# Two idle products of 512 columns around the first feed-forward unit of a hybrid encoder layer

## The chip, the cores and the metric

The kernel runs on one core of one Trainium2 chip. The metric is the device time of one execution in microseconds; the kernel before takes 914.95 us (median of 3 runs, 914.04 to 915.56). All matrices are float32. The engines named below are PE (TensorE, the matrix unit; its weight loads are listed as PEld), DVE (VectorE), ACT (ScalarE), POOL (GpSimd) and SP (SyncE, which issues most transfers).

## What is computed

One layer over 512 tokens of width 1024: two parallel mixers merged by gates, cross-attention over 256 memory tokens, and a gated feed-forward of width 2816. The change sits between the cross-attention and the feed-forward.

```python
def swiglu(hn, w_gate, w_up, w_down):
    return (jax.nn.silu(hn @ w_gate) * (hn @ w_up)) @ w_down
...
        merged = gate_a * (ya @ w_proj_a[i]) + gate_b * (yb @ w_proj_b[i])
        h = h + merged @ w_out[i]
        h = h + memory_cross_attention(rms_norm(h, xattn_norm_g[i]), memn,
                                       w_q[i], w_k[i], w_v[i], w_xo[i])
        h = h + swiglu(rms_norm(h, ffn_norm_g[i]), w_gate[i], w_up[i], w_down[i])
    return rms_norm(h, final_norm_g)
```

## The kernel before, in words

**Products.** Every float32 matrix is split into a rounded high part and a low part (`split`, L85 on ACT for the high part, L86 on DVE for the low one), and each product of two blocks is made as three PE products: high by high, high by low, low by high. Where the moving operand has all 512 tokens (or 512 weight columns), a PE product is 128x512; where it has half of the tokens, it is 128x256. The weights of a PE product are loaded by a load of its own (PEld), which runs while the product before it streams.

**Normalisation and turning.** Behind the attention's output projection each block of 128 token rows is added to the residual `h`, scaled to unit size, and turned on the PE so that features lie on partitions: `norm_feat` scales, and `to_feat` (L506) makes 8 transposes of 128x128 in two groups of four, each group into an auxiliary PSUM buffer `ptr`. ACT casts the group to the high part, DVE makes the low part, and ACT copies it once more into `full` (L510) for later sums. There are three auxiliary PSUM buffers (pool `paux`, tag `aux`), taken in turn; whoever takes one waits until the last reader of its former content is done. `to_feat` is not called at once but is put off with `later`, and `tick` calls it when the products issued since then amount to the time given. So the turning of the fourth and last block of rows falls into the first products of the feed-forward.

**Feed-forward.** The first 2560 columns of the gate and up projections are made in ten units of 512 columns. A unit multiplies a 2x2 block matrix by a 2x2 block matrix in seven jobs instead of eight (`product`, L1273), each job being 24 PE products of 128x256 on sums and differences of token blocks and weight blocks (numbered 1 to 7). The remaining 256 columns are made directly (`feat_block`, L350), in part among the first unit's jobs and the turning. The order of the jobs around the change is: half of the direct gate product and job 1 of the first gate unit (`px`), the rest of the gate product's first half, job 2 (`pv`), the gate product's second half, the direct up projection (`feat`, which takes two auxiliary PSUM buffers `pf0`, `pf1`), and then the loop over units, whose first pass begins with job 5 (`pq`), then job 6 (`px`), the next unit's jobs 1 and 2, and jobs 7, 4 and 3. Between job 5 and job 6 of the first pass one block of the normalised rows, `fn_hi` and `fn_lo` of the first four feature blocks and the last 256 tokens, is rewritten by a difference of blocks (`split(*fn_q(K0, T1), s3)`).

**Order.** Each engine works its own queue in order. A scheduler may reorder instructions within a queue except those marked `in_order`, which keep the program's order among themselves. Weights come by transfers from a plan that is issued a fixed number of jobs ahead; neither transfers nor plan are touched by the change.

**Names.** `ot_hi` holds the high part of the attention's output (features by tokens, 8 blocks of 512 tokens), complete long before the turning; its place is taken over by the feed-forward's gated values afterwards. `aux` gives an auxiliary PSUM buffer. `idles` at the start of the kernel makes small PE products whose results nobody reads, while the first transfers are under way. `NT - 1` is the last block of rows.

Of the kernel before, what the change touches and what calls it, by code (L numbers as in the profile page):

```python
# [17 lines left out]
P = 128  # L18
D = 1024
T = 512  # L20
NT = T // P
# [31 lines left out]
def hybrid_layer_kernel(  # L53
# [8 lines left out]
    nc = tc.nc  # L62
    x, mem, out = x[0], mem[0], out[0]
# [13 lines left out]
    def bank(name):  # L77
        return pm.tile([P, 512], F32, tag="mm", name=name)

    def aux(name, shape=(P, 512)):  # L80
        return pa.tile(list(shape), F32, tag="aux", name=name)

    def split(dst_hi, dst_lo, src):

        hi = nc.scalar.copy(dst_hi, src)  # L85
        lo = nc.vector.tensor_tensor(dst_lo, src, dst_hi.bitcast(F32), ALU.subtract)  # L86
        if pinned[0]:
            in_order(hi)
            in_order(lo)
# [3 lines left out]
    in_order = tc.keep_in_program_order  # L93
# [228 lines left out]
    def next_w(*key):  # L322
        i = used_w[0]
        used_w[0] += 1
        assert len(plan[i][0]) == len(key) and plan[i][0][1:] == key[1:] and plan[i][0][0] is key[0]
        for j in range(i, min(i + FAR + 1, len(plan))):
            begin(j, i)
            if j - 1 >= len(tiles) and j - 1 <= i + SPLITS:
                split_w(j - 1)
        for j in range(len(tiles), min(i + SPLITS + 1, len(plan))):  # L330
            split_w(j)
        tile_, tiles[i] = tiles[i], None
        return tile_
# [98 lines left out]
    def later(n, fn):  # L432

        side["later"].append((side["now"] + n, fn))
# [7 lines left out]
    def tick(us=5.2):  # L442

        side["now"] += us / 5.2
        run_due()
        side["credit"] = min(side["credit"] + us * side["rate"], us)
        while side["credit"] > 0.0 and side["gen"] is not None:
            try:
                used = next(side["gen"])
            except StopIteration:  # L450
                side["gen"] = None
                return
            if used is None:
                side["credit"] = 0.0
                return
            side["credit"] -= used

    def gain(src, name):
        t = np_.tile([P, D], F32, tag="gain", name=name, bufs=2)
        nc.sync.dma_start(t, src.partition_broadcast(P))  # L460
        return t

    ident = cp.tile([P, P], F32, name="ident")
# [6 lines left out]
    def sum_sq(dst, src):  # L470
        sq = np_.tile([P, 512], F32, tag="ev", name="sq", bufs=2)
        act = nc.scalar.activation(sq[:, :src.shape[-1]], src, AF.Square, accum_out=dst)
        if pinned[0]:
            in_order(act)
# [13 lines left out]
    def row_sums(src):  # L488
        ss = np_.tile([P, 2], F32, tag="ss", name="ss", bufs=2)
        for i in range(2):  # L490
            sum_sq(ss[:, i:i + 1], src[:, HALF[i]])
        return ss

    def rms_scale(src, g, dst, ss=None):

        r = rms_factor(row_sums(src) if ss is None else ss)
        for i in range(2):
            nc.vector.scalar_tensor_tensor(dst[:, HALF[i]], src[:, HALF[i]], r, g[:, HALF[i]], ALU.mult, ALU.mult)

    def to_feat(src, hi, lo, tsl, full=None, skip=None, part=(0, 1)):  # L500

        for q in part:
            ps = aux("ptr", (P, 4, P))
            for j in range(4):
                k = 4 * q + j
                nc.tensor.transpose(ps[:, j, :], src[:, k * P:(k + 1) * P], ident)  # L506
            if q != skip:
                split(hi[:, 4 * q:4 * q + 4, tsl], lo[:, 4 * q:4 * q + 4, tsl], ps)
            if full is not None:
                nc.scalar.copy(full[:, 4 * q:4 * q + 4, tsl], ps)  # L510

    xsp = [None]

    def norm_feat(src, g, hi, lo, tsl, ss=None, full=None, skip=None):
        xs = xsp[0].tile([P, D], F32, tag="xs", name="xs", bufs=2)
        rms_scale(src, g, xs, ss)
        later(0.6, lambda: to_feat(xs, hi, lo, tsl, full, skip))

    def slot(tag, shape, dt, name):
        return sp.tile(list(shape), dt, tag=tag, name=name)  # L520

    def token_slot(name, off=(0, 0)):

        return halves_at(sp.tile([P, 2 * KD * T + 128], F32R, tag="B", name=name), KD, T, off)
# [50 lines left out]
    ss = row_sums(xt[:, 1, :])  # L575
    for t in range(1, NT):
        rms_scale(xt[:, t, :], g_mix, xt[:, t, :], ss)
        if t == 1:
            ss = row_sums(xt[:, 2, :])
# [4 lines left out]
        if t == 2:  # L584
            ss = ss3
# [445 lines left out]
    for h in range(H):  # L1031
        ps = bank("psv")
# [22 lines left out]
    part = slot("A", (P, KD, T), F32, "part")  # L1055
# [91 lines left out]
    def add_evac(half, layer, fin, fin0=None):  # L1147

        def f(t, ps):
            nc.vector.tensor_tensor(h[:, t, HALF[half]], h[:, t, HALF[half]], ps, ALU.add)  # L1150
            sum_sq(hss[:, layer, t, half:half + 1], h[:, t, HALF[half]])
            if half == 1:
                fin(t, hss[:, layer, t, :])
            elif fin0 is not None:
                fin0(t)
        return f

    def feat_norm(g, hi, lo, full=None, skip=False):

        return lambda t, ss: norm_feat(h[:, t, :], g, hi, lo, slice(t * P, (t + 1) * P), ss, full,  # L1160
                                       0 if skip and t >= 2 else None)

    mg = (mg_hi, mg_lo)
    for half in range(2):
# [99 lines left out]
    def product(ps, u, q, start, ops):  # L1264

        hi, lo = next_w(u[0], u[1], q)
        for j in range(2):
            cs = slice(j * P, (j + 1) * P)
            for k in range(4):
                a = (hi[:, k, cs], lo[:, k, cs])  # L1270
                b = (ops[q][0][:, k, :], ops[q][1][:, k, :])
                for i, (x, y) in enumerate(((0, 0), (0, 1), (1, 0))):
                    nc.tensor.matmul(ps[:, j, :], a[x], b[y], start=start and j == k == i == 0,  # L1273
                                     stop=k == 3 and i == 2, skip_group_check=True)
        tick(2.7)

    def unit_bank(name):
        return bank(name).rearrange("p (j t) -> p j t", j=2)
# [61 lines left out]
    ot_hi = slot("D", (P, KD, T), F32R, "ot_hi")  # L1340
# [9 lines left out]
    g_f = gain(ffn_norm_g[0], "g_f")  # L1350
    ot = (ot_hi, ot_lo)
    fn_hi, fn_lo = token_slot("fn", APART)
# [9 lines left out]
    full = fp.tile([P, KD, T], F32, tag="full", name="full", bufs=1)  # L1362


    fin = add_evac(1, 1, feat_norm(g_f, fn_hi, fn_lo, full))
    held = []
    for t0 in (0, 2):
        ps = {t: bank(f"pt{t - t0}") for t in (t0, t0 + 1)}
# [51 lines left out]
    def sum4():  # L1420
        V.tensor_tensor(a12, a12, a11, ALU.add)
        make_op(3, 4, a12)
# [4 lines left out]
    def unit_start(u):  # L1427
        x, v = unit_bank("px"), unit_bank("pv")
        product(x, u, 1, True, ops)
        nc.scalar.copy(v, x)  # L1430
        return x, v
# [14 lines left out]
    ps = [bank("pf0"), bank("pf1")]  # L1446
# [61 lines left out]
    def down_product(ps, q, start, chunks=range(CHUNKS)):  # L1508
        for c in chunks:
            rows_product(ps, q, c, next_w(w_down, q, c), (0, 1), slice(0, 512), start and c == 0, c == CHUNKS - 1)  # L1510

    for i, u in enumerate(UNITS):
        final = i == len(UNITS) - 1
        x, v = begun
        q = unit_bank("pq")
        product(q, u, 5, True, ops)
        if final:
            last_job.append(u)
            make_tokens(1, 0)
        if i == 0:  # L1520
            split(*fn_q(K0, T1), s3)
        product(x, u, 6, False, ops)
        u2 = stp[0].tile([P, 2, 256], F32, tag="u2", name="u2", bufs=2)
        u3 = np_.tile([P, 2, 256], F32, tag="ev", name="u3", bufs=2)
        nc.scalar.copy(u2, x)
        if not final:
            begun = unit_start(UNITS[i + 1])
        else:
            dx = [bank(f"dx{t}") for t in range(2)]
            down_product(dx, 1, True, range(2))  # L1530
        product(x, u, 7, False, ops)
        nc.scalar.copy(u3, x)  # L1532
        if i == 0:
            sum4()
        if not final:
            unit_second(UNITS[i + 1], begun[1])
        V.tensor_tensor(u3, q, u3, ALU.subtract)
        put(u, 1, T1, u3)
        product(x, u, 4, False, ops)
        put(u, 0, T1, x)  # L1540
        if u[0] is w_up:
            a_, b_ = (acts(u[1] // 512, f)[:, :, T1] for f in (0, 1))
            V.tensor_tensor(a_, a_, b_, ALU.subtract)
        product(q, u, 3, False, ops)
        V.tensor_tensor(u2, q, u2, ALU.subtract)
        put(u, 1, T0, u2)
# [91 lines left out]
    for i in range(2):  # L1638
        p = aux("pcut", (P, 256))
# [37 lines left out]
```

## Time and profile before

| | before |
|---|---|
| time, median of 3 runs | 914.95 us (914.04 to 915.56) |
| span of the profiled execution, its own time | 915.4 us |
| weight loads (PEld) busy | 87% of the span |
| PE idle, waiting for ACT or DVE, from 589 to 800 us | none listed |
| DMA, mean | 168 GB/s |
| value projection of the attention (512 columns) | 443 to 465 us |
| query product (256 columns) | 466 to 507 us |
| turning of the last rows in front of the feed-forward | 586.4 to 587.4 us |
| units of the feed-forward (256 columns) | 608 to 804 us |
| down projection, its long run of 512 columns | 810 to 891 us |

A profile row of the timeline gives the start in us, the duration in us, the engine, the line, the operation, what is written and read, the shape and how many instructions are merged into the row. A record of a PE product is longer than its distance to the next one, because products overlap in the array; the pace has to be read from the starts, or from how many records fit into a stretch.

### The profile page before, as it was taken

Reading aid. Unit: us, or ns where it says so; the run is one execution under the profiler, and the core shown is the slowest. Engines: PE = TensorE matmul, PEld = TensorE weight load, DVE = VectorE, ACT = ScalarE, POOL = GpSimd, SP = SyncE. Lnnn points to the kernel's source line nnn. Section 1 sums busy time; section 2 is a strip of 40 time slices with the busy share of each in tenths; the row PEclk is TensorE's granted clock in tenths of the full one; section 3 lists DMA queues with packets and bytes.
Section 4 is the critical chain, followed back from the end, with each engine's and each line's share of the span. In section 5 each row is a group of like instructions: output and inputs, shape, how many; then the busy total and the mean of one; then the engine's idle time right before and its main releaser. Section 6 shows DMA issues by size and latency. Waiting matters only on the chain.

```text
span 915.4 us, 14510 instructions
## 1 busy us (share of the span) xinstructions
PE 900.7 (98%) x5650; PEld 796.5 (87%) x5650; DVE 623.8 (68%) x1018; ACT 475.4 (52%) x696; POOL 102.1 (11%) x161
## 2 busy tenths in 40 slices
PE   9999999999999999999999999999999999999996
PEld 6888888888888887789899878999999999988885
DVE  5696662888753236858956836776778767899875
ACT  5542985144364334447655634745455454655664
POOL 1004420110025200101000001100020100000000
PEclk9999999999999999999999999999999999999999
DMA  8456574685546577863578416526788873246672
GB/s 252 148 148 185 124 181 141 174 193 149 153 134 146 127 219 206 275 198 120 175 216 252 139 47 184 161 88 149 189 202 212 221 186 93 69 138 200 191 244 90
DMA packets 111974, 153.80 MB, mean 168 GB/s; under 512 B 13521, under 2 KB 78561, under 8 KB 111842
## 3 DMA queue, kind: packets, MB, share of 16 engines
q1 hardware_dynamic: 93026, 128.27, 44.1%
q0 software_dynamic: 16288, 23.57, 15.9%
q10 hardware_dynamic: 2592, 1.05, 0.5%
q8 instruction: 44, 0.72, 0.3%
q14 instruction: 24, 0.20, 0.1%
HBM read 146.08 MB, written 38.24 MB: 201 GB/s over the span
## 4 chain that ended last, share of the span: by engine, by line
PE 90%; ACT 4%; DVE 3%; issue 1%; POOL 0%; DMA 0%; POOLq 0%; SPq 0%; DVEq 0%; ACTq 0%
PE pf L350 27%; PE pt L350 16%; PE px L1273 12%; PE pq L1273 6%; PE dx L350 6%; PE dq L350 3%; PE pv L1273 3%; PE qx L1273 2%; PE dv L350 2%; PE pk L786 2%; PE ptr L506 1%; PE qq L1273 1%; DVE wlo L86 1%; PE po L350 1%; ACT whi L85 1%
## 5 line engine op out<-in xcount | busy, mean ns | idle before, releaser
L86 DVE TENSOR_TENSOR wlo<-wraw,whi 128x1024 fp32r<-128x1024 f32 (+1 forms) x139 | 164.9, 1187 | 109.5 <-ACT whi L85 107.8
L85 ACT CAST whi<-wraw 128x1024 fp32r<-128x1024 f32 (+1 forms) x139 | 142.2, 1024 | 163.0 <-PE pf L350 67.0
L350 PE MATMUL pf<-xn,whi 128*128 128x512 f32 x448 | 140.1, 392 | 0.0
L350 PEld LDWEIGHTS pf<-xn,whi 128*128 128x128 f32 x448 | 83.5, 188 | 17.0 <-issue 0.2
L350 PE MATMUL pf<-xn,wlo 128*128 128x512 f32 x224 | 87.4, 390 | 0.0
L1273 PE MATMUL px<-fn,whi 128*128 128x256 f32 x480 | 86.2, 281 | 0.0
L1273 PEld LDWEIGHTS px<-fn,whi 128*128 128x128 f32 x480 | 73.4, 188 | 0.3 <-ACT u L1532 0.2
L86 DVE TENSOR_TENSOR wlo<-b,whi 128x1024 fp32r<-128x1024 f32 x40 | 48.9, 1222 | 32.8 <-ACT whi L85 32.8
L85 ACT CAST whi<-b 128x1024 fp32r<-128x1024 f32 x40 | 42.0, 1051 | 56.2 <-PE px L1273 28.9
L1273 PE MATMUL px<-fn,wlo 128*128 128x256 f32 x240 | 67.5, 281 | 0.0
L1273 PE MATMUL pq<-s,whi 128*128 128x256 f32 x320 | 57.0, 281 | 0.0
L350 PE MATMUL dx<-whi,s 128*128 128x512 f32 x170 | 53.8, 391 | 1.4 <-ACT whi L85 1.0
L86 DVE TENSOR_TENSOR wlo<-t,whi 128x1024 fp32r<-128x1024 f32 x30 | 36.7, 1224 | 20.9 <-ACT whi L85 20.9
L85 ACT CAST whi<-t 128x1024 fp32r<-128x1024 f32 x30 | 31.5, 1051 | 36.8 <-PE pv L1273 13.3
L350 PEld LDWEIGHTS pf<-xn,wlo 128*128 128x128 f32 x224 | 42.1, 188 | 8.7
L1273 PEld LDWEIGHTS pq<-s,whi 128*128 128x128 f32 x320 | 48.9, 188 | 0.1
L1273 PEld LDWEIGHTS px<-fn,wlo 128*128 128x128 f32 x240 | 46.0, 192 | 0.0
L1273 PE MATMUL pq<-s,wlo 128*128 128x256 f32 x160 | 45.0, 281 | 0.0
L350 PE MATMUL pt<-whi,xn 128*128 128x512 f32 x128 | 42.6, 405 | 0.0
L350 PEld LDWEIGHTS dx<-whi,s 128*128 128x128 f32 x170 | 31.7, 188 | 8.3 <-ACT whi L85 1.2
L350 PE MATMUL dx<-wlo,s 128*128 128x512 f32 x85 | 33.2, 391 | 0.4 <-DVE wlo L86 0.4
L1273 PEld LDWEIGHTS pq<-s,wlo 128*128 128x128 f32 x160 | 30.7, 192 | 0.0
(414 smaller groups left out, 2235.4 us busy)
## 6 DMA issues: line engine op xcount, KB each, us to landing
wraw<-in_w_in_dram SPq DMA_DIRECT2D x36, 512.0 KB, 3.8
dsum<-in_w_down_dram SPq DMA_DIRECT2D x20, 512.0 KB, 6.7
wraw<-dsum SPq DMA_DIRECT2D x20, 512.0 KB, 4.4
b<-in_w_gate_dram SPq DMA_DIRECT2D x15, 512.0 KB, 4.6
b<-in_w_up_dram SPq DMA_DIRECT2D x15, 512.0 KB, 4.6
wraw<-in_w_down_dram SPq DMA_DIRECT2D x15, 512.0 KB, 3.7
dsum<-in_w_down_dram POOLq DMA_DIRECT2D x10, 512.0 KB, 6.8
dsum<-dsum POOLq DMA_DIRECT2D x10, 512.0 KB, 7.4
```

The lines of the kernel that those rows point to most:

```text
L85: hi = nc.scalar.copy(dst_hi, src)
L86: lo = nc.vector.tensor_tensor(dst_lo, src, dst_hi.bitcast(F32), ALU.subtract)
L350: nc.tensor.matmul(ps, a[x], b[y], start=start and i == 0, stop=stop and i == 2, skip_group_check=free)
L506: nc.tensor.transpose(ps[:, j, :], src[:, k * P:(k + 1) * P], ident)
L786: nc.tensor.matmul(ps[32 * j:32 * j + 32, q, :], bd[i][:, g].rearrange("p d c -> p (d c)"), lc(es[i], g), start=(i == 0), stop=False, tile ...
L1273: nc.tensor.matmul(ps[:, j, :], a[x], b[y], start=start and j == k == i == 0, stop=k == 3 and i == 2, skip_group_check=True)
```

## The change

A helper `long_idle` makes one PE product of 128x512 from a tile's first 128 columns as weights and its first 512 columns as the moving operand, into an auxiliary PSUM buffer that nobody reads. It is called in two places: at the end of `to_feat` for the last block of rows in front of the feed-forward, on `ot_hi`, where the transposes of this block are also marked to keep the program's order; and in the first pass over the units, between the rewriting of `fn` and job 6, on `fn_hi`. The computed result is the same.

```diff
+    def long_idle(x):
+
+        p = aux("long")
+        in_order(nc.tensor.matmul(p, x[:, 0, 0:P], x[:, 0, :], start=True, stop=True))
+
-    def to_feat(src, hi, lo, tsl, full=None, skip=None, part=(0, 1)):
+    def to_feat(src, hi, lo, tsl, full=None, skip=None, part=(0, 1), behind=None):
...
-                nc.tensor.transpose(ps[:, j, :], src[:, k * P:(k + 1) * P], ident)
+                tr = nc.tensor.transpose(ps[:, j, :], src[:, k * P:(k + 1) * P], ident)
+                if behind is not None:
+                    in_order(tr)
...
+        if behind is not None:
+            long_idle(behind)
...
-    def norm_feat(src, g, hi, lo, tsl, ss=None, full=None, skip=None):
+    def norm_feat(src, g, hi, lo, tsl, ss=None, full=None, skip=None, behind=None):
...
-        later(0.6, lambda: to_feat(xs, hi, lo, tsl, full, skip))
+        later(0.6, lambda: to_feat(xs, hi, lo, tsl, full, skip, behind=behind))
...
-    def feat_norm(g, hi, lo, full=None, skip=False):
+    def feat_norm(g, hi, lo, full=None, skip=False, behind=None):
...
-                                       0 if skip and t >= 2 else None)
+                                       0 if skip and t >= 2 else None, behind if t == NT - 1 else None)
...
-    fin = add_evac(1, 1, feat_norm(g_f, fn_hi, fn_lo, full))
+    fin = add_evac(1, 1, feat_norm(g_f, fn_hi, fn_lo, full, behind=ot_hi))
...
         if i == 0:
             split(*fn_q(K0, T1), s3)
+            long_idle(fn_hi)
         product(x, u, 6, False, ops)
```

## The prediction

> **What bounds the kernel now.** I read the page first, then the busy windows of the TensorE (PE) for stretches that hold only one kind of product, then the timeline around the two places of the change, last the waits of the feed-forward.
>
> ```profile
> span 915.4 us, 14510 instructions
> PE 900.7 (98%) x5650; PEld 796.5 (87%) x5650; DVE 623.8 (68%) x1018; ACT 475.4 (52%) x696; POOL 102.1 (11%) x161
> PEclk9999999999999999999999999999999999999999
> PE 90%; ACT 4%; DVE 3%; issue 1%; POOL 0%; DMA 0%; POOLq 0%; SPq 0%; DVEq 0%; ACTq 0%
> ```
>
> PE is busy 98% of the span and makes 90% of the chain that ended last, with the clock fully granted in every slice. So time can be won only by fewer products or by a shorter distance from one product to the next. That distance is not the same everywhere. Each row below is one stretch; its columns are the window, its length, PE's busy time with the number of records that touch it, the granted clock, the DMA engines' busy share and GB/s.
>
> ```profile
> 428.10:431.10 3.00, 3.00 (x29) 1.00 0.70 201
> 432.60:443.30 10.70, 10.70 (x93) 1.00 0.52 162
> 444.10:465.00 20.90, 20.90 (x91) 1.00 0.61 193
> 466.40:500.90 34.50, 34.50 (x307) 1.00 0.80 239
> 578.20:580.80 2.60, 2.60 (x24) 1.00 0.00 0
> 589.10:611.00 21.90, 21.90 (x188) 1.00 0.24 46
> 611.00:791.90 180.90, 180.90 (x1538) 1.00 0.69 170
> 807.20:809.90 2.70, 2.70 (x25) 1.00 0.50 123
> 810.00:891.00 81.00, 81.00 (x360) 1.00 0.67 204
> ```
>
> ```profile
> L1273 PE MATMUL qx<-hn,whi x96: 276/276/287, 465.7 to 507.0; 128*128 128x256 f32 x96
> L1273 PE MATMUL px<-fn,whi x480: 277/281/297, 578.4 to 804.6; 128*128 128x256 f32 x160
> ```
>
> A record lasts longer (276 or 281 ns) than the distance to the next, so a window touches one record's length more than it holds: distance = (window + record) / count. For products of 256 columns this is (34.50 + 0.276) / 307 = 113.3 ns in the query product stage, but (180.90 + 0.281) / 1538 = 117.8 ns in the feed-forward, and (21.90 + 0.281) / 188 = 118.0 ns in front of it. Both stages run the same helper, L1273, with weights from the same pool and rows in the same slot, at a granted clock of 1.00. Load on the DMA engines is no cause: the stretch of narrow distance has 0.80, the wide one of 578.20 has 0.00. The first two rows are the clue: both lie in the key projection, the same line and tiles, yet 428.10 has (3.00 + 0.276) / 29 = 113 ns (a short count, good to some 2 ns), and 432.60 has (10.70 + 0.281) / 93 = 118.1 ns, where the narrow distance would have fitted 97. What lies between them is only a turning of rows on the PE, after which the wide distance stays for 93 products. So there seem to be two paces, a narrow and a wide one, which an interruption sets and which then last. Products of 512 columns have two as well: (20.90 + 0.397) / 91 = 234 ns against (81.00 + 0.389) / 360 = 226 ns (0.397 and 0.389 are such records' lengths in the timeline).
>
> **The change part by part.** It removes nothing and moves no work. Instruction by instruction the queues of ACT, DVE, POOL and SP stay as they are, no DMA is added, and the PE gets two products of 128x512, whose results nobody reads. Holding the transposes in program order leaves them where they were.
>
> The first idle product comes six products into the second gate product (`pv`), behind the turning of the last 128 rows:
>
> ```profile
> 587.04 0.60 PE L506 MATMUL ptr<-ident,xs 128*128 128x128 f32 x4
> 587.39 1.19 PE L350 MATMUL pf<-fn,s 128*128 128x256 f32 x8
> 588.42 0.28 PE L1273 MATMUL pv<-fn,whi 128*128 128x256 f32 x1
> 591.24 5.82 PE L350 MATMUL pf<-fn,s 128*128 128x256 f32 x48
> 596.90 0.40 PE L350 MATMUL pf<-fn,whi 128*128 128x256 f32 x2
> ```
>
> Six products of 118 ns after 588.42 put it at 589.13. The row of 48 products gives the wide pace once more, (596.90 - 591.24) / 48 = 117.9 ns. The second one stands between job 5 and job 6 of the first unit, at 611.03:
>
> ```profile
> 610.91 0.28 PE L1273 MATMUL pq<-s,wlo 128*128 128x256 f32 x1
> 611.03 0.40 PE L1273 MATMUL px<-s,whi 128*128 128x256 f32 x2
> 586.26 0.58 ACT L510 COPY full<-ptr 128x512 f32<-128x512 f32 x1
> 588.33 1.27 ACT L510 COPY full<-ptr 128x512 f32<-128x512 f32 x2
> 606.41 1.05 ACT L85 CAST fn<-s 128x1024 fp32r<-128x1024 f32 x1
> ```
>
> Their own cost: one more place in the stream each, 226 to 234 ns by the two paces above, and the load of its weights lies under the product before it. Two make 0.46 us, all on the path.
>
> Their waits: the first needs the third auxiliary PSUM buffer back, whose last reader is the copy that ends at 586.26 + 0.58 = 586.84, 2.3 us before it. The up projection's two buffers move on by one in the ring: their last readers end at 588.33 + 1.27 = 589.60 and the first product of the up projection is at 596.90, 7.3 us later. The second reads rows that ACT has just rewritten; that cast ends at 606.41 + 1.05 = 607.46, 3.6 us before 611.03. I cost these waits at nothing. If ACT fell behind by more than those margins, everything on the PE's queue would stand behind the idle product for the excess, and the next unit's casts, which wait for the PE, with it; the trace shows nothing that would move ACT by microseconds.
>
> Their effect on the pace is the one large term, and the trace does not show a single product of 512 columns inside a wide stream of 256. If the narrow pace is reached and lasts, each later product of 256 columns saves 117.8 - 113.3 = 4.5 ns. From the second idle product to the end of the stretch there are 1538 - 2 = 1536 of them: 6.9 us. From the first there are 186 more: 7.7 us. The other bound is no gain, and below that a loss (third rival). The nearest rows for either bound are the changes from 512 to 256 columns:
>
> ```profile
> 465.26 0.40 PE L350 MATMUL pt<-wlo,mn_hi 128*128 128x512 f32 x1
> 465.50 0.39 PE L350 MATMUL pt<-whi,mn_lo 128*128 128x512 f32 x1
> 465.73 0.41 PE L1273 MATMUL qx<-hn,whi 128*128 128x256 f32 x2
> 465.97 0.28 PE L1273 MATMUL qx<-hn,wlo 128*128 128x256 f32 x1
> 466.09 0.39 PE L1273 MATMUL qx<-hn,whi 128*128 128x256 f32 x2
> 466.31 0.28 PE L1273 MATMUL qx<-hn,wlo 128*128 128x256 f32 x1
> 797.20 0.39 PE L350 MATMUL dx<-whi,s 128*128 128x512 f32 x1
> 797.42 0.40 PE L1273 MATMUL px<-fn,whi 128*128 128x256 f32 x2
> 797.66 0.28 PE L1273 MATMUL px<-fn,wlo 128*128 128x256 f32 x1
> ```
>
> At 465.73 a wide stream (233 ns per 512) turned narrow within five products (0.24 us for the first two, 0.22 for the last two). At 797.42 a stream of 512 products was followed by wide ones (0.24 us for two), and so it was at 807.20, (2.70 + 0.281) / 25 = 119 ns. So a 512 product does not set the narrow pace in every case. I take the gain: 465.73 is the nearest row in kind (the same helper, wide before it, as here), there are two tries, and nothing from 466.40 to 500.90 lost the narrow pace again over a dozen jobs of 24 products.
>
> What the faster stage would press on: casts and subtractions for the next weights.
>
> ```profile
> DVE wlo L86 <- ACT whi L85: 52.5, 46, 3.2
> ACT whi L85 <- PE px L1273: 35.2, 24, 2.0
> ```
>
> These are waits inside 589 to 800 (total us, times, longest): ACT stands waiting for the PE to give a weight buffer back, DVE for ACT, and no row there has the PE waiting. 7 us less over 200 us is 3.5%, well inside that idle time.
>
> Sum for the profiled execution: 915.4 + 0.46 - 7.7 = 908.2 if the first idle product sets the pace, 915.4 + 0.46 - 6.9 = 909.0 if only the second does. I take the middle, 908.6. The median of the runs, 914.95, lies 0.45 below that execution, so the forecast is 908.1.
>
> **The rivals.**
>
> Nothing but the cost. The wide pace is stable against a single 512 product: 797.42 and 807.20 speak for this, both in the feed-forward, where the three entries shown (578.20, 797.42, 807.20) came out wide; 465.73 speaks against. Time: 914.95 + 0.46 = 915.4. The same holds if the second product undoes at 611.03 what the first won: 186 x 4.5 ns = 0.8 us, net -0.4 us, 914.6.
> A rule points this way: the Trainium skill, "TensorE: Matmul & The Clock Gate", section "Step-by-step: what each phase is for", says that loading the next weights takes no read bandwidth from the running matmul, so there would be no pace to set. By the Trainium skill's section "Back-to-back issue gap" on that page, N/2.4 + 2.5 ns, 256 columns would take 109 ns always and two idle products of 512 together 0.43 us, an estimate that gives 915.4; the 113.3 and 117.8 ns of the rows above fit neither, so the rule is not the whole story here.
>
> Part of the way. The narrow pace is set and lost again at some unit. Against it: the wide stretch of 1538 records shows no disturbance at any unit's border. Half of the gain would give 914.95 + 0.46 - 3.8 = 911.6.
>
> Slower. The idle products leave the 256 stream wide, and shift the phase so that the down projection, now at 226 ns, enters the 234 ns pace in which the value projection (444.10) ran through all its 91 products. Price: 358 x (234 - 226) ns = 2.9 us, with the idle products 914.95 + 0.46 + 2.9 = 918.3. It decides from 810 on, where the down projection's long run of 512 columns follows the last product of 256. Against it: that entry is made today from a wide 256 stream (807.20) and ends at 226.
>
> **How the numbers follow.** Narrow pace from one of the idle products on: 0.51, 908.1. Part of the way: 0.10. Nothing but the cost, or undone: 0.23. Slower: 0.15. The rest, 0.01, is a wait that I have not seen. Differences below 0.2% (1.8 us) cannot be told from no change here, since three runs of one kernel spread over 1.5 us. So faster 0.61, same 0.23, slower 0.16. The likeliest case's own range is 907.0 to 909.3 (both sums less 0.45, and half a run's spread). The full range must take in "nothing but the cost" with its spread: 907.0 to 916.0, leaving out the slower case.
>
> **What would show it.** Right: in the changed profile products of 256 columns of the same helper lie 113.3 ns apart with records of 276 ns instead of 281, from 589.4 or 611.3 on; the unit stretch shrinks from 180.9 us to 174; two records of 128x512 without a wait in front. Wrong in the cause: records of 281 ns and 117.8 ns behind both, a span of 915.9. Wrong in the waits: an idle time on the PE ahead of either idle product that ACT ends. Slower rival: the window of the down projection with 397 ns records and 234 ns distance.

## The result, and the profile after

The changed kernel takes 907.62 us (median of 4 runs, 906.93 to 908.78); the kernel before, run beside it, 914.7 us (4 runs, 914.04 to 915.56). The ratio is 0.9924, with a 95% interval of 0.9913 to 0.9936: 5.8 to 8.0 us faster. The forecast was 908.1. Here and below the ratios are given as they were recorded; they are not the quotients of the medians beside them, which lie inside the same intervals.

The page of the changed kernel, span and busy engines; behind it the clock row and the chain of waits by engine:

```profile
span 905.5 us, 14515 instructions
PE 891.1 (98%) x5652; PEld 788.6 (87%) x5652; DVE 624.2 (69%) x1018; ACT 476.2 (53%) x696; POOL 101.4 (11%) x161
PEclk9999999999999999999999999999999999999999
PE 90%; ACT 3%; DVE 2%; DMA 2%; issue 1%; SPq 1%; POOL 0%; POOLq 0%; DVEq 0%; ACTq 0%
```

PE made two products more and was busy 9.6 us less, at the same granted clock. So time was won on the PE itself, and the busy windows say where (window, length, PE's busy time with the records that touch it, clock, DMA share, GB/s):

```profile
464.50:499.00 34.50, 34.50 (x307) 1.00 0.86 264
586.20:608.10 21.90, 21.90 (x187) 1.00 0.22 43
608.90:782.30 173.40, 173.40 (x1532) 1.00 0.70 175
800.50:881.50 81.00, 81.00 (x360) 1.00 0.64 205
```

Distances are read as in the prediction, (window + one record) / count. Queries: 34.776 / 307 = 113.3 ns, as before. Between the two idle products: (21.90 + 0.281) / 187 = 118.6 ns, still the wide pace. Behind the second: (173.40 + 0.276) / 1532 = 113.4 ns, the narrow one, to the end of the units. Down projection: (81.00 + 0.389) / 360 = 226 ns, as before. A count is good to one record, 0.6 ns in 187. The starts of products are sharper: from 586.20 to 608.10 there are 186 products, 117.7 ns each, and from 608.34 to 782.43 there are 1536, 113.3 ns each (starts from the timeline and the table below).

The timeline of the changed kernel's PE around the two idle products (start in us, duration, operation, merged instructions):

```profile
585.85 0.28 PE L1282 MATMUL pv<-fn,wlo 128*128 128x256 f32 x1
585.97 0.39 PE L503 MATMUL long<-ot_hi 128*128 128x512 f32 x1
586.20 0.40 PE L1282 MATMUL pv<-fn,whi 128*128 128x256 f32 x2
...
607.98 0.28 PE L1282 MATMUL pq<-s,wlo 128*128 128x256 f32 x1
608.10 0.40 PE L503 MATMUL long<-fn 128*128 128x512 f32 x1
608.34 0.40 PE L1282 MATMUL px<-s,whi 128*128 128x256 f32 x2
608.58 0.28 PE L1282 MATMUL px<-s,wlo 128*128 128x256 f32 x1
608.69 0.39 PE L1282 MATMUL px<-s,whi 128*128 128x256 f32 x2
608.92 0.28 PE L1282 MATMUL px<-s,wlo 128*128 128x256 f32 x1
```

The first idle product holds its place for 0.23 us and nothing changes behind it. The second holds it for 0.24 us, and the next steps shrink at once: two products in 0.24, two in 0.23 (608.69 to 608.92). The tile view gives their records in ns, 389 for the first and 398 for the second, and lists no idle time before either:

```profile
L503 PE MATMUL long<-ot_hi x1: 389/389/389, 586.0 to 586.0; 128*128 128x512 f32 x1
L503 PE MATMUL long<-fn x1: 398/398/398, 608.1 to 608.1; 128*128 128x512 f32 x1
```

Where the 9.9 us between the two profiled spans come from, by the starts of the same product in both timelines:

| product | before, us | after, us | after - before |
|---|---|---|---|
| a `pt` product of the first mixer | 20.00 | 18.18 | -1.82 |
| last one ahead of the first idle product | 589.00 | 585.85 | -3.15 |
| first one behind the first idle product | 589.13 | 586.20 | -2.93 |
| first one behind the second | 611.03 | 608.34 | -2.69 |
| first `dx` behind the units | 791.94 | 782.43 | -9.51 |

The first and the last line stand in the timeline of the kernel before as

```profile
20.00 0.39 PE L350 MATMUL pt<-wlo,xn 128*128 128x512 f32 x1
...
791.94 0.39 PE L350 MATMUL dx<-whi,s 128*128 128x512 f32 x1
```

and in that of the changed kernel as

```profile
18.18 0.39 PE L350 MATMUL pt<-wlo,xn 128*128 128x512 f32 x1
...
782.43 0.39 PE L350 MATMUL dx<-whi,s 128*128 128x512 f32 x1
```

The units give -9.51 + 2.69 = -6.82 us. The two idle products take 0.46. What lies ahead of the first idle product, -3.15, has nothing to do with the change: the PE's products there are the same in the same order. Of this, 1.82 us is there at 20 us and comes from the start of the kernel (see the last section); most of the rest comes in waits of the attention, where the difference goes from -1.89 at 516 us to -3.07 at 522 us. So the change itself is worth 6.82 - 0.46 = 6.36 us in this pair of profiles; the medians differ by 7.08.

### The profile page after: what moved, and what is told of

It is laid out like the page before. It is cut to its first block, busy times and chain, and to the rows that moved or that the text cites. A ratio compares the mean times of both kernels' runs of the same rounds, so it can differ in the third digit from the quotient of the medians.

```text
span 905.5 us, 14515 instructions
## 1 busy us (share of the span) xinstructions
PE 891.1 (98%) x5652; PEld 788.6 (87%) x5652; DVE 624.2 (69%) x1018; ACT 476.2 (53%) x696; POOL 101.4 (11%) x161
## 4 chain that ended last, share of the span: by engine, by line
PE 90%; ACT 3%; DVE 2%; DMA 2%; issue 1%; SPq 1%; POOL 0%; POOLq 0%; DVEq 0%; ACTq 0%
PE pf L350 27%; PE pt L350 16%; PE px L1282 12%; PE dx L350 6%; PE pq L1282 6%; PE dq L350 3%; PE pv L1282 3%; PE qx L1282 2%; PE dv L350 2%; PE pk L795 2%; PE po L350 1%; PE qq L1282 1%; PE ptr L511 1%; DMA slab<-in_s_log_step_dram 1%; PE psc L350 1%
## 5 line engine op out<-in xcount | busy, mean ns | idle before, releaser
L1282 PE MATMUL px<-fn,whi 128*128 128x256 f32 x480 | 83.3, 276 | 0.0
L350 PEld LDWEIGHTS pt<-whi,xn 128*128 128x128 f32 x128 | 24.2, 191 | 6.8 <-ACT xn L85 1.2
```

What stands on the lines that cost most here:

```text
L350: nc.tensor.matmul(ps, a[x], b[y], start=start and i == 0, stop=stop and i == 2, skip_group_check=free)
```

## The experiments

Two questions were left by the profile. Does the first idle product do anything, or prepare the second? And why does one set the pace and the other not: is it the place, or the operand? The two differ in both. In the kernel `ot_hi` begins at the start of its slot. `fn_hi` and `fn_lo` share a slot: by `APART = (48, 112)` the first begins 48 words (of 4 bytes) into it and the second 112 words past word 4096. Starts are counted this way below, as 0, 48 and 112; 4096 is a multiple of 128. The traces hold no addresses, so these are starts within the slot.

**Each alone, and the operands exchanged.** Four kernels, against 13 runs of the kernel before (915.52 us, 913.33 to 916.86).

Second alone (e1):

```diff
-    fin = add_evac(1, 1, feat_norm(g_f, fn_hi, fn_lo, full, behind=ot_hi))
+    fin = add_evac(1, 1, feat_norm(g_f, fn_hi, fn_lo, full))
```

> Only the second idle product (in the first unit, on fn_hi), the first is taken out. Theory O (the operand decides: fn_hi starts 48 words behind the start of its slot, ot_hi at the start) and theory P (the place decides): the second alone does it all, record of the idle product near 397 ns with 236 ns to the next, then 113.3 ns for the 1536 products; 6.8 - 0.24 = 6.6 us less than before, 0.24 us less than the changed kernel. Theory B (the first prepares the second): the stretch stays at 117.8 ns, time as before plus 0.2 us.

Measured: 908.53 us (907.4 to 909.5), ratio 0.9915 (0.99 to 0.993). The window of this kernel's PE over the units:

```profile
609.60:782.80 173.20, 173.20 (x1531) 1.00 0.72 175
```

(173.20 + 0.276) / 1531 = 113.3 ns. The second idle product needs no first one.

First alone (e2):

```diff
         if i == 0:
             split(*fn_q(K0, T1), s3)
-            long_idle(fn_hi)
```

> Only the first idle product (behind the turning, on ot_hi), the second is taken out. All theories: the idle product takes 227 ns and the 256-column products stay at 117.8 ns up to the end of the units, time as before plus 0.23 us. If the first had a hidden use, the units would run at 113.3 ns all the same.

Measured: 914.8 us (913.55 to 916.42), ratio 0.9995 (0.9985 to 1.0006): no change. The same view, from the idle product to the end of the units:

```profile
586.50:788.90 202.40, 202.40 (x1721) 1.00 0.65 157
```

(202.40 + 0.281) / 1721 = 117.8 ns throughout. Wide, over 1721 records, though a product of 512 columns went ahead of them.

The first place with rows of `fn_hi` (e3; weights its first 128 columns, moving the first 256 tokens of its first two blocks), the second place left out:

```diff
-        in_order(nc.tensor.matmul(p, x[:, 0, 0:P], x[:, 0, :], start=True, stop=True))
+        in_order(nc.tensor.matmul(p.rearrange("p (a b) -> p a b", a=2), x[:, 0, 0:0 + P], x[:, 0:2, 0:0 + 256],
+                                  start=True, stop=True))
...
-    fin = add_evac(1, 1, feat_norm(g_f, fn_hi, fn_lo, full, behind=ot_hi))
+    fin = add_evac(1, 1, feat_norm(g_f, fn_hi, fn_lo, full, behind=fn_hi))
...
-            long_idle(fn_hi)
```

> Only the first idle product, at the same place, but on fn_hi: weights its first 128 columns, moving operand two feature blocks of 256 tokens (512 columns). Theory O: 236 ns to the next product, then 113.3 ns from there on, 1536 + 186 products; 7.7 - 0.24 = 7.4 us less than before, 0.5 to 1.0 us less than the changed kernel. Theory P: 227 ns and 117.8 ns, time as before plus 0.23 us.

Measured: 909.22 us (905.66 to 910.09), ratio 0.9916 (0.9895 to 0.9936). Windows behind the idle product, and its own record:

```profile
586.00:608.00 22.00, 22.00 (x196) 1.00 0.25 56
609.00:780.00 171.00, 171.00 (x1511) 1.00 0.72 175
```

```profile
L503 PE MATMUL long<-fn x1: 398/398/398, 585.3 to 585.3; 128*128 128x512 f32 x1
```

(22.00 + 0.276) / 196 = 113.7 ns in front of the loop, (171.00 + 0.276) / 1511 = 113.4 ns in it, with the 398 ns record of the second place. The place does not decide.

The second place, with both operands 80 columns further into `fn_hi`, so that they start at word 128 of the slot (e4; the first place is left out as in the first experiment, here and up to the better version below):

```diff
+        in_order(nc.tensor.matmul(p.rearrange("p (a b) -> p a b", a=2), x[:, 0, 80:80 + P], x[:, 0:2, 80:80 + 256],
```

> Only the second idle product, on fn_hi from column 80 on (weights 128 columns, moving two blocks of 256 columns), so that both operands start 128 words behind the slot's start and not 48. Theory O: 227 ns and the units stay at 117.8 ns. Theory P: 236 ns and 113.3 ns, as with the unshifted one.

Measured: 914.49 us in one run. The window of the units and the record:

```profile
609.00:789.00 180.00, 180.00 (x1531) 1.00 0.70 169
```

```profile
L503 PE MATMUL long<-fn x1: 389/389/389, 608.0 to 608.0; 128*128 128x512 f32 x1
```

(180.00 + 0.281) / 1531 = 117.8 ns, and the 389 ns of the first place. Same tile, same place, same size; only where its operands start in the partition differs, and the effect is gone. So it is its operand, and not its place, that makes the first idle product of the change useless; that it is the start of `ot_hi` and nothing else about that tile is inferred from this, no run moves `ot_hi` itself.

**Which operand, and does the size matter?** Three kernels with one run each, beside 915.38 us for the kernel before, changing one thing of the second place each: the moving operand alone at word 128 (e5); the weights alone at word 128 (e6); 256 moving columns instead of 512 (e7). The first two read their 512 columns as two blocks of 256, as e3 did, and not in one piece.

```diff
-        in_order(nc.tensor.matmul(p, x[:, 0, 0:P], x[:, 0, :], start=True, stop=True))
+        in_order(nc.tensor.matmul(p.rearrange("p (a b) -> p a b", a=2), x[:, 0, 0:0 + P], x[:, 0:2, 80:80 + 256],
...
+        in_order(nc.tensor.matmul(p.rearrange("p (a b) -> p a b", a=2), x[:, 0, 80:80 + P], x[:, 0:2, 0:0 + 256],
...
+        in_order(nc.tensor.matmul(p[:, 0:256], x[:, 0, 0:P], x[:, 0, 0:256], start=True, stop=True))
```

> Second place alone, weights from the start of fn_hi (48 words behind the slot's start), moving operand two blocks of 256 columns from column 80 on (128 words). If the moving operand's start decides (it streams while the next job's weights load): 227 ns, units at 117.8 ns, 912 to 915 us. If the weights' start decides: 236 ns, 113.3 ns, 6.6 us less than before.

> The opposite of e5: weights from column 80 on (128 words), moving operand from column 0 (48 words). If the moving operand's start decides: 236 ns, then 113.3 ns, 6.6 us less than before. If the weights' start decides: 227 ns and 117.8 ns.

> Second place alone, on fn_hi, but with 256 moving columns. If the width matters (only a product longer than the weight load shifts the loads against the streams): it is one more product of the wide stream, 118 ns, and the units stay at 117.8 ns, time as before. Rival: any foreign product breaks the pattern, then 113.3 ns and 6.7 us less than before.

Measured: 915.93, 906.77 and 914.29 us. The same window of each, moving shifted, weights shifted, 256 columns in this order:

```profile
612.00:780.00 168.00, 168.00 (x1428) 1.00 0.72 177
```

```profile
612.00:780.00 168.00, 168.00 (x1484) 1.00 0.72 175
```

```profile
612.00:780.00 168.00, 168.00 (x1429) 1.00 0.72 176
```

168.3 us over 1428, 1484 and 1429 records: 117.8, 113.4 and 117.8 ns. What decides between the first two is the moving operand's start, not the weights'; and a product of 256 columns does nothing, even with a start at which 512 columns work. The times are of one run each; it is the windows, over 1400 products each, that tell the cases apart.

**Which starts.** Two more of one run each (kernel before: 914.93 us, 913.48 to 916.15, 9 runs), again in the second place with the weights of `fn_hi`: moving rows of `fn_lo`, which start at word 112 (e11), and of `fn_hi` from column 32, word 80 (e12).

```diff
-        in_order(nc.tensor.matmul(p, x[:, 0, 0:P], x[:, 0, :], start=True, stop=True))
+        in_order(nc.tensor.matmul(p.rearrange("p (a b) -> p a b", a=2), x[:, 0, 0:P], fn_lo[:, 0:2, 0:256],
...
+        in_order(nc.tensor.matmul(p.rearrange("p (a b) -> p a b", a=2), x[:, 0, 0:0 + P], x[:, 0:2, 32:32 + 256],
```

> Second place alone, weights from the start of fn_hi, moving operand two blocks of 256 columns of fn_lo, which start 112 words behind a multiple of 128. If every start off a multiple of 128 words sets the narrow pace: 230 to 240 ns, then 113.3 ns. If 48 words is special: 227 to 230 ns, then 117.8 ns.

> As e11, moving operand fn_hi from column 32 on, 80 words behind a multiple of 128. If every start off a multiple of 128 words sets the narrow pace: 113.3 ns behind it. If 48 words is special: 117.8 ns.

Measured: 910.06 and 913.53 us. The window for word 112, then for word 80:

```profile
612.00:780.00 168.00, 168.00 (x1485) 1.00 0.73 179
```

```profile
612.00:780.00 168.00, 168.00 (x1429) 1.00 0.72 176
```

113.3 and 117.8 ns. Two simple rules fall: it is not that any start off a multiple of 128 words works (80 does not), and not that 48 is the only one (112 does). Of the five starts that were tried, 48 and 112 work; 0 (of `ot_hi`), 80 and 128 do not. One rival is left untested: 48 and 112 are also where the moving operands of the units' own products start (their sums and `fn` are all laid out by `APART`), so it may be agreement with these that counts and not the two places as such. A kernel with another `APART` would tell.

**A better version? (e8)** The third experiment, e3, showed one idle product on rows of `fn_hi` in the first place to be enough. The key projection, wide since the turning in its middle, can be given the same behind that turning, on `hn_hi`, which also starts at word 48:

```diff
-        tokm(w_out, half * 512, mg, KD, add_evac(half, 0, feat_norm(g_x, hn_hi, hn_lo, hfull, True)))
+        tokm(w_out, half * 512, mg, KD, add_evac(half, 0, feat_norm(g_x, hn_hi, hn_lo, hfull, True, behind=hn_hi)))
```

> As e3 (one idle product on fn_hi behind the turning in front of the feed-forward), and another of the same shape on hn_hi behind the last turning in front of the attention, in the key projection. If the start of the moving operand decides there as well: some 85 products of 256 columns at 113.3 and the value projection's 96 products of 512 at 226.7 in place of 233.3, 0.4 + 0.6 - 0.23 = 0.8 us less than e3. The rival that would eat it: the query products, now entered from a narrow stream, turn wide as at 797.42 and 807.20 in the profile before, up to 4.5 ns for each of 310 products, 1.4 us lost.

Measured: 907.59 us in one run. Windows of the key, value and query products, and the two idle products:

```profile
433.70:443.20 9.50, 9.50 (x86) 1.00 0.46 148
444.00:465.00 21.00, 21.00 (x94) 1.00 0.64 196
466.40:500.90 34.50, 34.50 (x307) 1.00 0.87 262
```

```profile
L503 PE MATMUL long<-hn x1: 392/392/392, 433.4 to 433.4; 128*128 128x512 f32 x1
L503 PE MATMUL long<-fn x1: 398/398/398, 587.6 to 587.6; 128*128 128x512 f32 x1
```

The key projection goes narrow, (9.50 + 0.276) / 86 = 113.7 ns; the value projection's 512-column products come out at (21.00 + 0.39) / 94 = 227.6 ns by the count, good to 2.4 ns. By the starts of the first and the last of its 96 products they go from 233.4 ns in the third experiment to 228.9 ns; the queries stay at 113.3, so the rival by which they would turn wide falls. Against the third experiment, product by product, this is worth 0.57 us by the end of the value projection: 0.39 over the key projection and 0.41 over the value projection, less 0.23 for the idle product. 0.8 had been expected, with the value projection at 226.7 ns; that is the term that fell short. No run here tried another start in the key projection, so that 48 is what matters there is not shown.

This same kernel (e9) and the changed one (e10) were then run together, five rounds each:

> The kernel of e8 again, timed: 7.4 us less than before for the feed-forward and 0.4 us for the key and value projections, 0.4 to 1.4 us less than the changed kernel (e10), which the spread of the runs may hide. If the extra gain seen in the profiles of e3 and e8 is not real, it is level with e10.

> The changed kernel as it is, as a base for e9: 6.4 us less than before by the sum of its parts (1536 x 4.45 - 0.46), 6.4 to 7.1 us less measured.

Measured: 906.12 us (905.35 to 908.74), ratio 0.9915 (0.9899 to 0.9931), against 909.41 us (908.94 to 910.03), ratio 0.9942 (0.9929 to 0.9956). The version with the idle products on `hn_hi` and `fn_hi` was the faster one here, but not all of the 3.3 us is its own: of the 3.9 us between the two profiles 2.1 are there at 19 us, before anything differs. The other 1.8 build up where they should: 0.80 over the key and value projections less 0.23 for the idle product there, 0.79 between the first and the second place, 0.24 at the second place, which has no idle product now, and 0.16 behind the units.

## Why the prediction was right, step by step

- *There are two paces of 113.3 and 117.8 ns, which an interruption sets and which last.* Held. 1532 records lie in one narrow stretch behind the second idle product, 1721 in one wide stretch without it; no unit's border, no DMA share from 0.22 to 0.87, changed a pace.
- *An idle product of 512 columns sets the narrow pace.* Held for the second, failed for the first. This is the step that was wrong in part: the sum took the middle between "the first sets it" (908.2) and "only the second does" (909.0, both for the profiled execution). Only the second did, so the first term of 7.7 us should have been 6.9, and the rival "nothing but the cost" is the true story of the first idle product. It treated the two as two tries of one thing; they differed in where the moving operand starts, which the text did not look at. That the second start was one that works was luck, seen from the prediction's reasons. Its sentence that a 512 product does not set the pace in every case was right; whether the operand's start is also the reason at 797.42 and 807.20, on which it rested, no run shows.
- *1536 products at 4.5 ns, 6.9 us.* Measured 6.82 us from the second idle product to the end of the units: 4.44 ns each.
- *Cost 226 to 234 ns each, 0.46 us together.* Measured 0.23 (wide stream on both sides) and 0.24 us.
- *The waits cost nothing.* Held: no idle time before either idle product. Inside 586 to 792 us, against 589 to 800 before, the waits on the weights' path are of like size (DVE for ACT 46.8 us after 52.5, ACT for the PE 33.5 after 35.2), and the one row that has the PE side waiting is 0.3 us:

```profile
DVE wlo L86 <- ACT whi L85: 46.8, 46, 3.2
ACT whi L85 <- PE px L1282: 33.5, 25, 1.9
...
PEld dx L350 <- DVE s L86: 0.3, 1, 0.3
```

- *Slower: the down projection goes to 234 ns.* It stayed at 226 ns; the rival fell.
- *Nothing but the cost, and the Trainium skill's rule beside it.* The Trainium skill ("TensorE: Matmul & The Clock Gate", section "Back-to-back issue gap") gives N/2.4 + 2.5 ns as the gap of an isolated product, and says that in a stream of loads and products both set the spacing; the prediction applied the formula to the stream. By the section "Step-by-step: what each phase is for" of the same page in the Trainium skill, the next weights' load takes no read bandwidth from the running product. The runs show what neither speaks of: 168 us hold 1428 or 1484 of the same products, by what one product ahead of them read.
- *The size of the sum.* "Only the second" gives 909.0 - 0.45 = 908.55; the second alone was measured at 908.53 (e1), the change at 907.62 and, in the repeat, at 909.41. That 907.62 lies so near to the 908.1 on record is luck and no merit of the middle: the start of the kernel alone moves an execution by more than the 0.8 us between the two sums (last section).

What stays open is the mechanism under the start of the operand. A product whose moving operand reads 512 columns from word 48 or 112 shifts the stream behind it into the narrow rhythm, and one from 0, 80 or 128 does not; that its reads meet those of the next weights' load in another order is a guess, which no run tests. The distance from the idle product to the next one was 233 to 237 ns where the pace turned in the feed-forward and 227 or 230 where it did not, yet in the key projection it turned after 230. So this distance is no sure sign of the pace behind it.

## What to carry to other kernels

Where the PE is the bound, work out the distance of equal products stage by stage, from records per window: here two stages of one helper that differed by 4% at a full clock showed a pace that could be set, and one product was worth 1500 times 4.5 ns. Set it with a product whose operands are laid out like those for which it is known to work, and try each inserted product alone: of the two in this change one earned everything and the other only cost its 0.23 us. And before the gain is read off two profiles, subtract the difference that is there ahead of the change's first instruction.

## What the runs showed that was not expected

**The start of the kernel comes in two lengths.** The first products run at about half their pace, and for how long differs from execution to execution, in both kernels. The timeline's four `pg` products of the kernel before, and of the changed one, and the windows from 5 to 12 us in the same order:

```profile
5.63 3.78 PE L558 MATMUL pg<-g_row,ones 1*128 1x512 f32 x4
```

```profile
5.28 1.98 PE L567 MATMUL pg<-g_row,ones 1*128 1x512 f32 x4
```

```profile
5.00:12.00 7.00, 6.94 (x19) 1.00 1.00 362
```

```profile
5.00:12.00 7.00, 6.88 (x26) 0.76 0.95 347
```

The same four products take 3.78 or 1.98 us, and the two profiles are 2.7 us apart by 10.9 us. Part of it is given back, 1.82 us are left at 20 us. It is no effect of the change: the changed kernel's repeat has 19 records in that window, like the kernel before, and its 909.41 us against 907.62 go the same way.

The clock column needs care here. The trace's clock records begin only at 13.59 us in the kernel before and at 4.85 us in the changed one, and the view counts time without a record as 1.00. The products go by these times: the `pt` products of 512 columns before start 0.42 us apart at 13.00 and 0.24 us apart at 13.97. The 0.76 of the changed kernel is a recorded clock of 0.50 from 8.26 to 11.68 us. In the traces of all kernels here a full clock on record before 7 us is followed by such a dip, one from 13 us on is not. The mean clock that is recorded for every run differs with this, and the times go with it: of the 22 runs of the kernel before beside the experiments e1 to e4 and e9 to e12, the 8 at 0.996 or 0.997 took 913.33 to 914.70 us and the 14 at other values 914.93 to 916.86. Three of the four runs behind 907.62 were at 0.996 and none of the five behind 909.41, so the 1.8 us between these two medians of one kernel go with its start.

That the first microseconds of products run at a lower rate, and for a time that differs from run to run, is also what the Trainium skill says ("TensorE: Matmul & The Clock Gate", "What's actually happening"). The trace agrees in kind. The Trainium skill's figure there, about 3.4 us of sustained work, is near the changed kernel's execution, whose full clock is on record 3.8 us behind its first product at 1.06 us; it is far from the 12.5 us of the kernel before.

**The pace has more than two values for 512 columns.** By the starts of products it is 226.7 ns in the down projection, 233.4 in the value projection of the kernel before, and 228.9 in the value projection behind a narrow key projection.
